# A decoder step on one Trainium2 core: the convolution's running sum in PSUM, and layer A's weight residues on GpSimd

## The chip, the cores and the metric

The kernel runs on one core of a Trainium2 chip. The core has a matrix engine (TensorE, PE in the profile, its weight loads PEld), a vector engine (VectorE, DVE), a scalar engine (ScalarE, ACT), a general engine (GpSimd, POOL), and a queue engine (SyncE, SP) that issues DMAs. Each engine has its own instruction queue; semaphores order work between them. Matrix products land in PSUM (eight banks of 128 x 512 floats), everything else lies in SBUF. The metric is the device time of one launch in microseconds, the median of several runs. Smaller is better.

## What is computed

One inference step of a small decoder trunk, for 512 prompt tokens and 64 sample tokens (8 sequences of 8), 576 columns together, width 2048. Layer A is a Conformer convolution module, layer B a dilated sliding-window attention; both also attend to a memory of 256 positions. This is layer A:

```python
h = jnp.einsum('btd,de->bte', x, w_in)          # w_in: 2048 x 5632
ga, gb, gate, qm, gm = jnp.split(h, ...)        # 1536, 1536, 1536, 512, 512
u = ga * jax.nn.sigmoid(gb)
ext = jnp.concatenate([conv_prev, u], axis=1)   # 30 older rows ahead
conv = depthwise_conv(ext, w_dw, width=31) + b_dw
c = silu(layernorm(conv)) * silu(gate)
m = mem_attn(qm, mem_kv) * silu(gm)
y = jnp.einsum('bte,ed->btd', jnp.concatenate([c, m], -1), w_out)
x = layernorm(ALPHA * x + y)
```

Layer B is built in the same way, with attention in place of the convolution, and adds its relative-position bias from a table (`rel_bias`) to the logits.

## The kernel before

**Products in three passes.** Weights and activations are float32. Each is split into a high part, rounded to a format that TensorE multiplies in one pass, and a low part, the residue. A product is high x high + high x low + low x high. Activations are split once. Weights arrive from HBM as slabs: a *unit* is one slab of 128 output channels by all inputs, a *quarter* is 4 of its 16 blocks of 128 inputs (a 128x512 tile). For each quarter ScalarE writes the high part (`wh`, line 203, five buffers) and VectorE the low part (`wl = raw - wh`, line 214, four buffers).

**Order.** The program is written out by hand: on each engine, instructions run in the order in which the Python code issues them. `run_steps` (line 241) goes through the list of quarters. A step issues the quarter's matmuls (line 262), then hooks, then the high part of the quarter three steps ahead and the low part of the one two steps ahead (`issue_split`), then the evacuation of a unit that ended in the step before, then `stage_lanes` (line 219, one piece from each of three queues of generators), then *background* work from `bg`. How much background work a step issues is a budget, `state["avail"]`: a step adds the time of its columns, and each piece takes off a planned cost; a low part takes 0.6.

**Layer A's sequence** (line 26): 12 pairs of units gb and ga (`p`), 4 units qm, 8 memory units (`mk`, 256 columns), 4 gm, one gate, up to `n_seq` (line 790); then the other gates, then the output projection. At the end of ga number j, `ev_ga` (line 612) writes `ep` and `es` on VectorE, stores `es` to the output `o_cs` by a DMA from GpSimd's queue (line 622), and appends the convolution of 128 channels to `bg`: `first` (line 647), then 30 `tap`s (line 656). A tap is one VectorE instruction on 128x512, `conv = ep[k:] * w + conv` (line 662), in place in SBUF.

**The bias tables.** A hook at step 20, the first memory quarter, puts `bias_task` (line 517) into lane 2. All its DMAs go through GpSimd's queue: it fills two tables in HBM (lines 529 to 536), stores the rows of three groups four times each (line 550), and then for each of four heads copies them in shifted rows. The core of that is:

```python
for r in range(4):
    nc.gpsimd.dma_start(dram(tp_, o, ...), dram(sc[0], ...))            # line 557
    nc.gpsimd.dma_start(tp_[h, r, 0:32, 0:128], md[0:32, 0:128])        # line 559, over part of the same rows
...                                                                     # line 561, twice
yield
nc.gpsimd.dma_start(dram(tl_, o, ...), dram(sc[0], ...))                # line 567
...                                                                     # line 570, three times
yield
...                                                                     # lines 574 (twice) and 577
yield
```

**PSUM.** `pp` (two buffers of two banks) takes the units' products. `at` (line 101, four buffers of one bank) takes all small products: memory attention, transposes, sums over channels, bias rows.

Of the kernel before, what the change touches and what calls it, by code (L numbers as in the profile page):

```python
# [13 lines left out]
AF = mybir.ActivationFunctionType  # L14
OP = mybir.AluOpType
# [4 lines left out]
TP, TS = 512, 64  # L20
# [14 lines left out]
TAPS = 31  # L35
# [46 lines left out]
def trunk(ctx, tc, xt, memt, wm, wa, wao, wb, wbo, cst, scv, kc, rest, mc, relb, oneh,  # L82
          o_y, o_yf, o_cp, o_cs, o_kv, o_kvn, o_kc, o_rest, o_mem):
    nc = tc.nc
# [8 lines left out]
    def u(shape, dt=F32, name="u"):  # L93
        names[0] += 1
        return U.tile(list(shape), dt, tag="u", name=f"{name}{names[0]}")
# [5 lines left out]
    def at(shape=(128, 512)):  # L101
        names[0] += 1
        return psum.tile(list(shape), F32, tag="at", bufs=4, name=f"at{names[0]}")

    def cast(ap):
        return ap.bitcast(F32)
# [33 lines left out]

    steps, quarters, halves = [], [], []
    raws, splits = {}, {}
    state = dict(dma=0, hi=0, split=0, pos=0, avail=0.0, extra=0.0, cap=4.0)
    lanes = [deque(), deque(), deque()]
    bg = deque()
    hooks = {}
# [44 lines left out]
    def issue_hi(upto):  # L191
        while state["hi"] < min(upto, len(quarters)):
            i = state["hi"]
            un, q, hidx = quarters[i]
            issue_dma(hidx + 1)
            r = raws[hidx][q % 2]
            if un.keep:
                f_ = un.keep
                hi, lo = f_([128, 512], F32R, "keep"), f_([128, 512], F32R, "keep")
            else:  # L200
                hi = wpool.tile([128, 512], F32R, tag="wh", bufs=5, name=f"wh{i}")
                lo = None
            nc.scalar.copy(hi, r)  # L203
            splits[i] = (hi, lo, r)
            state["hi"] += 1

    def issue_split(upto):
        while state["split"] < min(upto, len(quarters)):
            i = state["split"]
            issue_hi(i + 1)  # L210
            hi, lo, r = splits[i]
            if lo is None:
                lo = wpool.tile([128, 512], F32R, tag="wl", bufs=4, name=f"wl{i}")
            nc.vector.tensor_tensor(lo, r, cast(hi), op=OP.subtract)  # L214
            splits[i] = (hi, lo)
            state["split"] += 1
            state["avail"] -= 0.6

    def stage_lanes():
        for ln in lanes:  # L220
# [72 lines left out]
    def cols(ps, n=288):  # L293
        return ps[:, :, 0:n]
# [295 lines left out]
    def sp_x(k):  # L590
        xh[k], xl[k] = split_f32r(xraw.pop(k), [128, T], "x")

    def x_ready(k, c):
        if xh[k] is None:
            sp_x(k)
# [4 lines left out]
    later, cst_ = {}, {}  # L600
# [10 lines left out]
    def ev_ga(j):  # L611
        def f(ps):
            ep = u([128, HIST + TP], name="ep")
            es = u([128, 8, HIST + 8], name="es")
            nc.vector.memset(ep[:, 0:HIST], 0.0)
            nc.sync.dma_start(es, scv[j])
            g = sg.pop(j)
            nc.vector.tensor_tensor(ep[:, HIST:].rearrange("p (c n) -> p c n", c=2), cols(ps, 256),
                                    g[:, 0:TP].rearrange("p (c n) -> p c n", c=2), op=OP.mult)
            nc.vector.tensor_tensor(es[:, :, HIST:], ps[:, 1, 256:320].rearrange("p (b s) -> p b s", b=8),  # L620
                                    g[:, TP:].rearrange("p (b s) -> p b s", b=8), op=OP.mult)
            nc.gpsimd.dma_start(o_cs[j], es)
            cv = convs[j] = u([128, T], name="conv")
            cs = cv[:, TP:]
            prod = {}

            def sample_tap(k, bias=None):

                g = min(k // 8, 3)
                if g not in prod:  # L630
                    prod[g] = u([128, 9, TS], name="prod")
                dst = prod[g][:, k - 8 * g + (1 if g else 0), :].rearrange("p (b s) -> p b s", b=8)
                w = dw[:, j * 31 + k:j * 31 + k + 1]
                if bias is None:
                    nc.scalar.activation(dst, es[:, :, k:k + 8], AF.Copy, scale=w)  # L635
                else:
                    nc.scalar.activation(dst, es[:, :, k:k + 8], AF.Identity, scale=w, bias=bias)

            def sample_sum(g):
                n = 9 if g in (1, 2) else 8  # L640
                if g == 0 and j > 1:
                    nc.scalar.activation(prod[0][:, 8, :], cst_["shift"][:, TP:], AF.Copy, scale=-1.0)
                    n = 9
                dst = cs if g == 3 else prod[g + 1][:, 0, :]
                nc.vector.reduce_sum(dst, prod.pop(g)[:, 0:n, :].rearrange("p k n -> p n k"), axis=AX.X)

            def first():
                w = dw[:, j * 31:j * 31 + 1]
                b = b_dw[:, j:j + 1]
                if j < 2:  # L650
                    nc.vector.tensor_scalar(cv[:, 0:TP], ep[:, 0:TP], w, b, op0=OP.mult, op1=OP.add)
                    return
                nc.scalar.activation(cv[:, 0:TP], cst_["shift"][:, 0:TP], AF.Identity, bias=b, scale=-1.0)
                nc.vector.scalar_tensor_tensor(cv[:, 0:TP], ep[:, 0:TP], w, cv[:, 0:TP], op0=OP.mult, op1=OP.add)

            def tap(k):
                w = dw[:, j * 31 + k:j * 31 + k + 1]
                for m in range((k - 4) * TAPS // 27, (k - 3) * TAPS // 27) if k >= 4 else ():
                    sample_tap(m, None if m else b_dw[:, j:j + 1])
                if k == 6:  # L660
                    nc.scalar.copy(cps[:, j, :], ep[:, TP:TP + HIST])
                nc.vector.scalar_tensor_tensor(cv[:, 0:TP], ep[:, k:k + TP], w, cv[:, 0:TP], op0=OP.mult, op1=OP.add)  # L662
            bg.append((0.67, first))
            rest_ = later.pop(j - 1, [])
            for k in range(1, TAPS):
                bg.append((0.67, lambda k=k: tap(k)))
                if k in (13, 20, 28):
                    bg.append((0.7, lambda g=(k - 12) // 7: sample_sum(g)))
                if k in (3, 5, 7, 9, 11) and rest_:
                    bg.append(rest_.pop(0))  # L670

            def shift():

                ps_ = colsum(cv)
                cst_["shift"] = u([128, T], name="shift")
                for c in range(2):
                    nc.vector.tensor_scalar(cst_["shift"][:, c * 288:(c + 1) * 288], ps_[c][:, :288], 1.0 / 128, None,
                                            op0=OP.mult)
                yield 0.75

            def shifted():
                nc.vector.tensor_tensor(cv, cv, cst_["shift"], op=OP.subtract)

            def square():
                cst_["sq"] = u([128, T], name="sq")
                nc.scalar.activation(cst_["sq"], cv, AF.Square)
                if j == 0:
                    cst_["s1"] = u([128, T], name="s1")
                    nc.vector.tensor_copy(cst_["s1"], cv)
                    cst_["s2"] = cst_.pop("sq")  # L690
                else:
                    nc.vector.tensor_tensor(cst_["s1"], cst_["s1"], cv, op=OP.add)

            def square2():
                nc.vector.tensor_tensor(cst_["s2"], cst_["s2"], cst_.pop("sq"), op=OP.add)
            last_sum = (0.7, lambda: sample_sum(3))
            todo = later[j] = [last_sum]
            if j == 0:
                todo.append((0.0, lambda: lanes[2].append(shift())))
            if j < 2:  # L700
                todo.append((0.67, shifted, lambda: "shift" in cst_))
            todo.append((0.67, square))
            if j:
                todo.append((0.67, square2))
        return f
# [64 lines left out]
    for it in seq:  # L770
# [11 lines left out]
        un = Unit(wa[row + j], KT, xh, xl, ch, ev(j), x_ready, cost=0.75 if kind == "ga" else 0.0)  # L782
# [6 lines left out]
        if kind == "ga" and j == NCT - 1:  # L789
            n_seq = len(steps)  # L790
# [698 lines left out]
    for e in range(KT - N_SPLIT, KT):  # L1489
# [3 lines left out]
        un = unit_last(e, [(FIRST, T - FIRST)], ev, 1.2)  # L1493
# [10 lines left out]
    n_end = len(steps)  # L1504


    def temp_pool():
        es_ = ExitStack()
        scopes["s"] = (es_, es_.enter_context(tc.tile_pool(name="spool2", bufs=4)))
# [14 lines left out]
        hooks.setdefault(n_mk - 10 + j, []).append(lambda j=j: sp_mem(j))  # L1524
    for k in range(4, KT):
        hooks.setdefault((k - 4) // 4 * 2 + 1, []).append(lambda k=k: x_ready(k, None))
    temp_pool()
    issue_dma(1)
    for k in range(KT):
# [181 lines left out]
```

## Time and profile before

| | us |
|---|---|
| median of 3 runs | 1817.6 |
| lowest, highest | 1812.64, 1824.57 |
| the profiled execution, device time | 1815.19 |
| its span, first to last instruction | 1813.4 |

The profile is one execution. Busy time says how long an engine was executing, an idle stretch is put down to what ended it, and the chain that ended last is followed back from the last instruction. On that chain TensorE has 97% of the span, of which the line of the units' matmuls (262) has 86%. VectorE is busy for 55%, ScalarE for 37%, GpSimd for 7%. In 40 slices of the span VectorE's busy tenths are 6 to 9 in the first 14 and 2 to 6 in most of the others.

### The profile page before, as it was taken

The page shows a single profiled execution, that of the slowest core. Times are in us where ns is not written, and L with a number is a line of the kernel's source. Part 1 is how long each engine was busy: PE and PEld are TensorE (multiplying, and loading weights), DVE is VectorE, ACT ScalarE, POOL GpSimd, SP SyncE. Part 2 cuts the span into 40 slices and gives each one's busy share as a digit, 9 for nine tenths or more (in the row PEclk, how much of TensorE's full clock was granted, in tenths as well). Part 3 has the DMA queues.
Part 4 walks back from the last instruction along what each step waited for, and adds up shares of the span by engine and source line. Part 5 has one row for each costly group of instructions (what it writes and reads, how often), then busy time and mean ns, then how long its engine had stood idle before and what let it go on. Part 6 is the DMA issues. An engine that isn't in the chain of part 4 may idle for free.

```text
span 1813.4 us, 34545 instructions
## 1 busy us (share of the span) xinstructions
PE 1799.5 (99%) x14374; PEld 1725.0 (95%) x14374; DVE 1003.8 (55%) x1739; ACT 670.9 (37%) x1544; POOL 119.9 (7%) x215
## 2 busy tenths in 40 slices
PE   8999999999999999999999999999999999999998
PEld 8999999999999999999999999988999988899997
DVE  6977988378999765546762233222322222225866
ACT  5454444355455442223562232222322212224334
POOL 0222221000000000000000000010000011100000
PEclk9999999999999999999999999999999999999999
DMA  8585777575655465565642343676566666842312
GB/s 304 182 265 169 233 231 268 173 244 189 207 197 194 155 223 187 171 224 206 198 157 82 117 140 117 210 247 250 186 214 223 198 241 232 286 158 60 115 48 105
DMA packets 83901, 344.87 MB, mean 190 GB/s; under 512 B 15823, under 2 KB 24047, under 8 KB 72352
## 3 DMA queue, kind: packets, MB, share of 16 engines
q1 hardware_dynamic: 60240, 249.48, 41.3%
q0 software_dynamic: 20048, 90.03, 14.1%
q10 hardware_dynamic: 3456, 3.15, 0.5%
q8 instruction: 113, 1.85, 0.4%
q14 instruction: 44, 0.36, 0.1%
HBM read 322.83 MB, written 114.42 MB: 241 GB/s over the span
## 4 chain that ended last, share of the span: by engine, by line
PE 97%; ACT 1%; DMA 1%; DVE 1%; issue 0%; ACTq 0%; SPq 0%; DVEq 0%
PE pp L262 86%; PE at L1203 1%; PE at L1148 1%; PE at L458 1%; PE at L436 1%; DMA raw<-wb 1%; PE at L1085 1%; PE at L1083 1%; PE at L503 0%; PE at L483 0%; PE at L1106 0%; PE at L451 0%; PE pp L880 0%; PE at L804 0%; PE at L1096 0%; PE at L1053 0%
## 5 line engine op out<-in xcount | busy, mean ns | idle before, releaser
L214 DVE TENSOR_TENSOR wl<-raw,wh 128x512 fp32r<-128x512 f32 x492 | 333.7, 687 | 295.6 <-PE pp L262 159.3
L203 ACT CAST wh<-raw 128x512 fp32r<-128x512 f32 x492 | 297.7, 618 | 492.5 <-PE pp L262 168.0
L262 PE MATMUL pp<-yh,wh 128*128 128x320 f32 (+2 forms) x1536 | 340.8, 304 | 0.0
L262 PE MATMUL pp<-yl,wh 128*128 128x320 f32 (+2 forms) x1536 | 329.5, 296 | 0.3 <-DVE yl L997 0.3
L262 PE MATMUL pp<-yh,wl 128*128 128x320 f32 (+2 forms) x1536 | 329.3, 296 | 0.0
L262 PE MATMUL pp<-xh,wh 128*128 128x288 f32 (+2 forms) x1408 | 307.5, 300 | 5.8 <-ACT xh L364 5.8
L262 PE MATMUL pp<-xh,wl 128*128 128x288 f32 (+2 forms) x1408 | 303.4, 297 | 0.0
L262 PE MATMUL pp<-xl,wh 128*128 128x288 f32 (+2 forms) x1408 | 303.4, 297 | 0.0
L262 PEld LDWEIGHTS pp<-yh,wh 128*128 128x128 f32 x1536 | 253.2, 189 | 27.7 <-ACT wh L203 13.4
L662 DVE SCALAR_TENSOR_TENSOR conv<-ep,consts,conv 128x512 f32<-128x512 f32 x360 | 269.7, 749 | 6.9
L262 PEld LDWEIGHTS pp<-yl,wh 128*128 128x128 f32 x1536 | 256.0, 189 | 0.7 <-DVE yl L997 0.7
L262 PEld LDWEIGHTS pp<-yh,wl 128*128 128x128 f32 x1536 | 256.0, 189 | 0.0
L262 PEld LDWEIGHTS pp<-xh,wh 128*128 128x128 f32 x1408 | 234.2, 191 | 8.9 <-ACT xh L364 5.8
L262 PEld LDWEIGHTS pp<-xl,wh 128*128 128x128 f32 x1408 | 234.1, 190 | 0.3 <-DVE xl L365 0.3
L262 PEld LDWEIGHTS pp<-xh,wl 128*128 128x128 f32 x1408 | 234.1, 190 | 0.0
L262 PE MATMUL pp<-cath,wh 128*128 128x288 f32 (+2 forms) x640 | 140.5, 297 | 0.0
L262 PE MATMUL pp<-catl,wh 128*128 128x288 f32 (+2 forms) x640 | 139.7, 296 | 0.0
L262 PE MATMUL pp<-cath,wl 128*128 128x288 f32 (+2 forms) x640 | 139.6, 296 | 0.0
L262 PEld LDWEIGHTS pp<-cath,wh 128*128 128x128 f32 x640 | 104.2, 189 | 0.8 <-issue 0.3
L262 PEld LDWEIGHTS pp<-catl,wh 128*128 128x128 f32 x640 | 104.1, 189 | 0.0
L262 PEld LDWEIGHTS pp<-cath,wl 128*128 128x128 f32 x640 | 104.1, 189 | 0.0
L635 ACT ACTIVATE prod<-es,consts 128x64 f32<-128x64 f32 x360 | 103.0, 343 | 1.3 <-ACT mkv L403 1.3
(281 smaller groups left out, 1838.3 us busy)
## 6 DMA issues: line engine op xcount, KB each, us to landing
o_kc<-kc SPq DMA_DIRECT2D x104, 512.0 KB, 5.7
kv<-kc POOLq DMA_DIRECT2D x52, 1024.0 KB, 5.4
raw<-wb SPq DMA_DIRECT2D x96, 512.0 KB, 4.1
raw<-wa SPq DMA_DIRECT2D x86, 512.0 KB, 4.5
o_rest<-rest SPq DMA_DIRECT2D x64, 512.0 KB, 6.3
kv<-mc POOLq DMA_DIRECT2D x16, 1024.0 KB, 6.9
raw<-wao SPq DMA_DIRECT2D x32, 512.0 KB, 4.5
raw<-wm SPq DMA_DIRECT2D x24, 512.0 KB, 4.8
```

Of the source, the lines that this page charges most:

```text
L203: nc.scalar.copy(hi, r)
L214: nc.vector.tensor_tensor(lo, r, cast(hi), op=OP.subtract)
L262: nc.tensor.matmul(un.ps[:, c, :n], w[wi], xs[k][:, c0:c0 + n], start=(k == 0 and a == 0), stop=(k == un.nk - 1 and a == 2 and not un.tail))
L436: nc.tensor.matmul(lg[:, a * 256:(a + 1) * 256], q[:, t0:t0 + 128], kt, start=True, stop=True)
L458: nc.tensor.matmul(o[:, 0:256], vt[:, kk, :], PT[:, kk * 256:(kk + 1) * 256], start=(kk == 0), stop=(kk == 1))
L635: nc.scalar.activation(dst, es[:, :, k:k + 8], AF.Copy, scale=w)
L662: nc.vector.scalar_tensor_tensor(cv[:, 0:TP], ep[:, k:k + TP], w, cv[:, 0:TP], op0=OP.mult, op1=OP.add)
L1083: nc.tensor.matmul(o, lhs, kk, start=True, stop=True, tile_position=(0, 32 * a))
L1085: nc.tensor.matmul(lg[:, 128 + 128 * g:256 + 128 * g], q_[g, h][:, r * 128:(r + 1) * 128], k_[g, h][:, r * 128:(r + 1) * 128], start=True, ...
L1148: nc.tensor.matmul(lg[32 * rg:32 * rg + 32, :], qe[g][:, rg * 128 + b * 32:rg * 128 + b * 32 + 32], ck[:, rg, :], start=(b == 0), stop=(b ...
L1203: nc.tensor.matmul(acc[32 * rg:32 * rg + 32, 0:128], pe[i % 2][:, rg * 128 + b * 32:rg * 128 + b * 32 + 32], cv[:, rg * 4 + b, :], start=( ...
```

## The change

- `conv`'s running sum is kept in a tile of `at`, one PSUM bank, from `first` to the last tap, which writes its result to the SBUF tile `conv`. `first`, on ScalarE and VectorE, writes PSUM too.
- `issue_split` issues the subtraction for the first `state["low"]` quarters on GpSimd in place of VectorE, and then takes nothing off `avail`. `halves_before(n_seq)` is the number of quarters up to `n_seq`.

```diff
-    state = dict(dma=0, hi=0, split=0, pos=0, avail=0.0, extra=0.0, cap=4.0)
+    state = dict(low=0, dma=0, hi=0, split=0, pos=0, avail=0.0, extra=0.0, cap=4.0)
...
-            nc.vector.tensor_tensor(lo, r, cast(hi), op=OP.subtract)
+            if i < state["low"]:
+                nc.gpsimd.tensor_tensor(lo, r, cast(hi), op=OP.subtract)
+            else:
+                nc.vector.tensor_tensor(lo, r, cast(hi), op=OP.subtract)
+                state["avail"] -= 0.6
             splits[i] = (hi, lo)
             state["split"] += 1
-            state["avail"] -= 0.6
...
+            acc = {}
...
             def first():
                 w = dw[:, j * 31:j * 31 + 1]
                 b = b_dw[:, j:j + 1]
+                ac = acc[0] = at()
                 if j < 2:
-                    nc.vector.tensor_scalar(cv[:, 0:TP], ep[:, 0:TP], w, b, op0=OP.mult, op1=OP.add)
+                    nc.vector.tensor_scalar(ac, ep[:, 0:TP], w, b, op0=OP.mult, op1=OP.add)
                     return
-                nc.scalar.activation(cv[:, 0:TP], cst_["shift"][:, 0:TP], AF.Identity, bias=b, scale=-1.0)
-                nc.vector.scalar_tensor_tensor(cv[:, 0:TP], ep[:, 0:TP], w, cv[:, 0:TP], op0=OP.mult, op1=OP.add)
+                nc.scalar.activation(ac, cst_["shift"][:, 0:TP], AF.Identity, bias=b, scale=-1.0)
+                nc.vector.scalar_tensor_tensor(ac, ep[:, 0:TP], w, ac, op0=OP.mult, op1=OP.add)
...
-                nc.vector.scalar_tensor_tensor(cv[:, 0:TP], ep[:, k:k + TP], w, cv[:, 0:TP], op0=OP.mult, op1=OP.add)
+                dst = acc[0] if k < TAPS - 1 else cv[:, 0:TP]
+                nc.vector.scalar_tensor_tensor(dst, ep[:, k:k + TP], w, acc[0], op0=OP.mult, op1=OP.add)
...
+    def halves_before(n):
+
+        return max(un.qi[q] for un, q, _, _ in steps[:n]) + 1
...
+    state["low"] = halves_before(n_seq)
```

## Rows read from the trace of the kernel before

**Rows 1.** The page, section 1: busy us, share of the span, instructions by engine.

```profile
PE 1799.5 (99%) x14374; PEld 1725.0 (95%) x14374; DVE 1003.8 (55%) x1739; ACT 670.9 (37%) x1544; POOL 119.9 (7%) x215
```

**Rows 2.** Waits of TensorE, whole span: waiter, releaser, us in total, times, longest.

```profile
PE pp L262 <- ACT xh L364: 5.8, 1, 5.8
PE pp L262 <- DVE wl L214: 1.2, 2, 1.0
PE at L388 <- ACT mkv L403: 0.7, 1, 0.7
```

**Rows 3.** Groups by line and shape, VectorE: busy us, mean ns, idle before.

```profile
L214 DVE TENSOR_TENSOR wl<-raw,wh 128x512 fp32r<-128x512 f32 x492 | 333.7, 687 | 295.6 <-PE pp L262 159.3 <-ACT wh L203 101.6 <-issue 34.3
L662 DVE SCALAR_TENSOR_TENSOR conv<-ep,consts,conv 128x512 f32<-128x512 f32 x360 | 269.7, 749 | 6.9
...
L890 DVE SCALAR_TENSOR_TENSOR r<-xl,r 128x576 f32<-128x576 f32 x15 | 11.4, 758 | 0.5
...
L889 DVE SCALAR_TENSOR_TENSOR r<-xh,pp 128x576 f32<-128x576 f32 x15 | 11.3, 755 | 31.1 <-PE pp L262 31.1
```

**Rows 4.** Windows: us, busy (instructions) PE PEld DVE ACT POOL, PEclk, DMA, GB/s.

```profile
115.00:120.00 5.00, 3.92 (x20) 3.72 (x21) 4.96 (x8) 3.34 (x9) 1.22 (x2) 0.70 0.39 93
...
150.00:200.00 50.00, 50.00 (x378) 50.00 (x377) 45.54 (x68) 21.71 (x62) 12.40 (x20) 1.00 0.63 201
450.00:500.00 50.00, 50.00 (x378) 50.00 (x377) 49.29 (x74) 22.43 (x66) 1.09 (x2) 1.00 0.62 206
```

**Rows 5.** Timeline of GpSimd: start us, us, what [idle before, and what ended it].

```profile
66.26 0.53 POOL L529 MEMSET mt<- 128x512 f32 x1
...
73.99 0.53 POOL L536 DMA_DIRECT2D tl__92<-md  x1
85.82 2.16 POOL L550 DMA_DIRECT2D bd<-bt  x4 [11.30 <-ACT bt L546]
...
94.84 0.74 POOL L557 DMA_DIRECT2D tp__91<-bd  x1 [0.19 <-issue]
...
120.89 0.50 POOL L559 DMA_DIRECT2D tp__91<-md  x1 [3.73 <-DMA tp__91<-bd]
...
123.62 0.57 POOL L567 DMA_DIRECT2D tl__92<-bd  x1
136.94 1.70 POOL L570 DMA_DIRECT2D tl__92<-bd  x3 [12.74 <-DMA tl__92<-bd]
...
144.81 0.72 POOL L557 DMA_DIRECT2D tp__91<-bd  x1
...
197.21 0.52 POOL L559 DMA_DIRECT2D tp__91<-md  x1 [3.11 <-DMA tp__91<-bd]
...
220.96 1.70 POOL L570 DMA_DIRECT2D tl__92<-bd  x3 [6.49 <-DMA tl__92<-bd]
225.70 1.09 POOL L574 DMA_DIRECT2D tl__92<-bd  x2 [3.04 <-DMA tl__92<-bd]
...
275.23 2.20 POOL L622 DMA_DIRECT2D o_cs<-es  x4
```

**Rows 6.** Waits of GpSimd, 60 to 280 us.

```profile
POOL tp__91 L559 <- DMA tp__91<-bd: 82.9, 16, 8.4
POOL tl__92 L570 <- DMA tl__92<-bd: 34.9, 4, 12.7
...
POOL tl__92 L574 <- DMA tl__92<-bd: 17.0, 4, 6.1
```

**Rows 7.** Groups by line, GpSimd.

```profile
L125 POOL MEMSET qe<- 128x512 f32 x3 | 1.4, 524 | 0.0
```

**Rows 8.** The chain that ended last, 60 to 135 us: start us, us, what.

```profile
90.01 17.47 PE pp L262 x144
```

**Rows 9.** Timeline of VectorE: `es` of the third pair.

```profile
153.58 0.21 DVE L620 TENSOR_TENSOR es<-pp,sg 128x64 f32<-128x64 f32 x1
```

**Rows 10.** Timeline of SyncE's queue: the first copies of `rest`.

```profile
121.20 13.03 SPq L354 DMA_DIRECT2D o_rest<-rest  x6
```

## The prediction

> **What bounds the kernel now.** I read the page first, for shares by engine. TensorE's matmuls fill 99% of the span [rows 1], so the question is only whether something holds it up. The waits of TensorE come next: 5.8 us on the first cast of x, 1.2 us in all on VectorE's low parts, 0.7 us on a small product, nothing else of size [rows 2]. So the 333.7 us that VectorE spends on low parts [rows 3] are almost wholly hidden. Then the windows: in a stretch of plain quarters TensorE gets through 378 matmuls in 50 us whether VectorE is busy for 45.5 us of it or for 49.3 [rows 4]; at 24 matmuls to a quarter that is 3.17 us a quarter. VectorE is nearly full there, and still not the bound.
>
> The view that decides is the last one I read, GpSimd's timeline, because a second engine is about to be put on TensorE's supply line. GpSimd is busy for only 119.9 us [rows 1], but what matters in an in-order queue is when it is blocked. From 94.84 to 275.23 us it works through one chain, the copies of the bias tables (lines 557 to 577): issue a DMA, wait until it has landed, issue the next one onto the same rows. In its first head the copies of line 567 (123.62) are followed by a wait of 12.74 us; the second head begins at 144.81 [rows 5]. Of these 180.4 us, 82.9 + 34.9 + 17.0 = 134.8 us are such waits [rows 6], and the other 45.6 us are issuing. Now it costs nothing, since only o_cs stores and later loads stand behind it.
>
> **What is taken from VectorE.** `low` is the number of quarters up to `n_seq`: 12 pairs of ga and gb (96 quarters), qm, gm and one gate (36), and the 8 memory units (32), together 164. So 164 subtractions of 687 ns [rows 3], 112.7 us, leave VectorE, and `avail` is no longer charged 0.6 for each. TensorE waited 1.2 us for them in the whole run, so what can be won is that 1.2 us and part of the lull at 115 to 120 us, where 20 matmuls ran in 5 us [rows 4] against the 38 of the usual pace (18 x 0.13 = 2.4 us).
>
> **The running sum in PSUM.** 360 taps of 749 ns [rows 3], with 12 first terms, now read and write a PSUM bank. Reading: the two lines 889 and 890 are the same operation on 128x576, one with its second input in PSUM and one wholly in SBUF, and take 755 and 758 ns [rows 3]: no surcharge. [...] Writing PSUM from VectorE is in no row; I bound it between nothing and the 62 ns by which line 662 exceeds line 214, the largest surcharge between two-input rows of 512 columns [rows 3]. I take nothing; at the upper bound 372 x 0.062 = 23 us go back to VectorE, less than the 112.7 it is rid of. One of the four `at` banks is now held for 31 taps at a time; users of the other three are the memory attention's small matmuls, whose readers run a step ahead.
>
> **The subtraction on GpSimd.** No row shows a two-input operation there. The nearest is its MEMSET of 128x512, 524 ns [rows 7], one write and no input. I bound the subtraction from below by this and from above by three such passes (two reads, one write), 1.57 us, and take the middle, 1.1 us. A plain quarter leaves 3.17 us, so it keeps up there. A quarter of a memory unit leaves 1.46 us (144 matmuls, which are 12 quarters of 12, in 17.47 us [rows 8]), so it just keeps up there too; at 1.57 us the 19 memory quarters outside the chain would cost 2 us.
>
> **What stands in front of it.** This is where the change costs. A low part is issued two steps ahead of its quarter, and `stage_lanes` runs behind it in the same step. `bias_task` joins lane 2 at step 20, the first memory quarter, and gives out one piece a step. Counting its yields, GpSimd's queue becomes: low 28, the fill of `md` and eight copies, low 29, four bias stores, low 30, four, low 31, four, low 32, then for each of four heads the piece of line 557 to 561 (four waits), a low part, lines 567 and 570 (one wait), a low part, lines 574 and 577 (one wait), a low part; the last piece stands before low 44. Each quarter's third pass needs its low part, so TensorE may not pass quarter 33 until head 1's first piece is through, and so on. That the queue doesn't let later work by is in the rows: `es` of the third pair was written at 153.58 us [rows 9], yet the stores of pairs three to six were issued back to back at 275.23 us, as soon as the chain had ended [rows 5].
>
> The price, first part: the fill piece takes from 66.26 to 74.52 us, 8.3 us, and the bias stores 12 x 0.54 = 6.5 us [rows 5]; their wait for ScalarE before 85.82 us falls away, since by then TensorE has passed that product. With four subtractions (4.4) this is 19.2 us, while TensorE has four quarters of 1.46 (5.8) and a lead: with four `wl` buffers GpSimd is at most three quarters ahead, less the subtraction, 3.3 us. Stall 10 us.
>
> Second part, the chain: 45.6 us of issuing plus the waits. How long are those, when TensorE crawls? The smallest of each kind in the trace are 3.11 us (line 559), 6.49 (line 570) and 3.04 (line 574) [rows 5]; 16 x 3.11 + 4 x 6.49 + 4 x 3.04 = 88 us against 134.8. They were measured under traffic of some 200 GB/s [rows 4]. In the stalled stretch there is next to none: twelve quarters of weights (256 KB each) in some 140 us are 22 GB/s, and the o_rest copies, first issued at 121.20 us [rows 10], belong to steps behind the memory units. So I go near the smallest, 90 us, and the chain takes 135.6. Of the 12 subtractions in it, the two thirds that stand in front of a wait run while that DMA lands, so they add 4 x 1.1 = 4.4. TensorE does its 12 quarters within, 17.5 us. Stall 135.6 + 4.4 - 17.5 = 122.5 us.
>
> [...]
>
> Sum, against the profiled execution: 1815.2 + 10 + 122.5 = 1947.7, say 1948 us. The median of the three runs is 2.4 us above that execution, which is nothing beside the bounds. Everything behind `n_seq` stays as it is, later.
>
> Bounds of the unknown: waits as long as before and no subtraction hidden, 10 + 180.4 + 13.2 - 17.5 = 186 us, 2001 us; waits half their smallest (44), 10 + 45.6 + 44 + 4.4 - 17.5 = 87 us, 1902 us. With no wait at all, issuing alone would still be 45.6 + 13.2 - 17.5 = 41 us.
>
> **Rivals.** *The waits don't shrink* (the copies with their many short rows are slow by themselves): 2001 us. For it, between 115 and 120 us traffic was down to 93 GB/s [rows 4], and the wait of line 559 that ended at 120.89 us still took 3.73 us [rows 5]; against it, that is already below their mean of 82.9 / 16 = 5.2 [rows 6]. *They shrink far more*: 1902 us.
>
> *The shared port.* Taps with both tensors in SBUF and a GpSimd subtraction may block each other. With the sum in PSUM a tap has one SBUF input left. If it still shut out and was shut out by the subtraction, VectorE would get 1.1 us per quarter back for the 0.69 it lost; in the stretch where it is full (from 450 us on, the last 47 quarters or so before `n_seq` [rows 4]) it would fall 19 us behind, o_cs would hold the low parts behind it, and the time would be 1967 us. Nothing in the trace of before shows the two together. [...]
>
> *The other side: the low parts are not held up*, because the queue lets them pass the waiting copies, or because the pieces end up elsewhere. Then only the gains remain, 1815.2 - 1.2 - 2.4 = 1812 us, no change that can be measured. It would need the copies to take less than the 17.5 us that TensorE has for the twelve quarters; their issuing alone takes 45.6, and the stores at 275.23 us speak against passing.
>
> **How the numbers follow.** The forecast (a stall of 105 to 170 us) 0.63; waits unshrunk 0.13; far shorter waits 0.11; the port on top of the stall 0.06; no stall 0.07. The predicted time is the forecast's, 1948 us. The range runs from a little below the short waits to a little above the unshrunk ones, 1895 to 2010, and leaves out the last case and part of the port. About 1% is what a measurement of this kernel can tell from no change: slower by over 1% 0.93, within 1% 0.05, faster 0.02.
>
> **What would show it.** Right: between roughly 90 and 230 us TensorE idle for over 100 us, waiting for GpSimd's `wl`, and GpSimd waiting for DMAs of lines 559, 570 and 574 in between; the quarter pace of 3.17 us before and behind it; the granted clock low inside. Wrong: TensorE's waits for `wl` near zero, or `wl` written in time while the bias copies are pending; then the order in the queue is not what I counted. If the subtraction takes over 3.2 us, all of layer A is paced by it, and the time is far above the range. If taps are longer than 811 ns, writing PSUM costs more than I allow.

## The result, and the profile after

The changed kernel takes 1954.97 us (median of 4 executions, 1949.19 to 1966.91), the kernel before in the same session 1815.74. The ratio is 1.0767, 95% interval 1.0703 to 1.0831: slower by 139 us. The prediction was 1948, in a range of 1895 to 2010. The profiled execution of the changed kernel is the longest of its four; the last section says where its last 10 us went.

The page of the changed kernel, busy time by engine, and two rows of its 40 slices (compare [rows 1]):

```profile
PE 1831.9 (93%) x14374; PEld 1747.4 (89%) x14374; DVE 921.9 (47%) x1575; ACT 671.6 (34%) x1544; POOL 336.8 (17%) x379
...
PE   8932299999999999999999999999999999999999
...
PEclk9955599999999999999989999999999999999997
```

VectorE is busy for 82 us less, GpSimd for 217 more, and no engine is anywhere near full except TensorE. The loss stands in slices 3 to 5, 98 to 246 us: there TensorE is busy for 2 or 3 tenths. The waits of TensorE and of GpSimd (waiter, releaser, us in total, times, longest) say for what:

```profile
PE pp L265 <- POOL wl L215: 114.0, 15, 21.7
PE pp L265 <- ACT xh L367: 6.5, 2, 6.3
PE pp L265 <- DVE wl L217: 3.1, 3, 1.9
```

```profile
POOL tp__91 L562 <- DMA tp__91<-bd: 59.0, 16, 5.0
POOL o_cs L625 <- DVE es L623: 49.4, 9, 14.0
...
POOL tl__92 L573 <- DMA tl__92<-bd: 20.4, 4, 5.8
...
POOL tl__92 L577 <- DMA tl__92<-bd: 1.3, 2, 0.7
```

TensorE, which in [rows 2] waited for nothing of size, now waits 114 us for low parts written by GpSimd; GpSimd in turn stands at the same waits for landed copies as in [rows 6] (lines 559, 570 and 574 are now 562, 573 and 577). GpSimd's timeline puts the two together (start, duration, what, idle before and what ended it):

```profile
95.63 0.55 POOL L536 DMA_DIRECT2D tl__92<-md  x1 [5.27 <-DMA md<-mt]
...
111.18 0.74 POOL L560 DMA_DIRECT2D tp__91<-bd  x1
116.94 0.51 POOL L562 DMA_DIRECT2D tp__91<-md  x1 [5.01 <-DMA tp__91<-bd]
...
133.35 1.27 POOL L215 TENSOR_TENSOR wl<-raw,wh 128x512 fp32r<-128x512 f32 x1
134.55 0.58 POOL L570 DMA_DIRECT2D tl__92<-bd  x1
140.72 1.70 POOL L573 DMA_DIRECT2D tl__92<-bd  x3 [5.59 <-DMA tl__92<-bd]
142.44 1.27 POOL L215 TENSOR_TENSOR wl<-raw,wh 128x512 fp32r<-128x512 f32 x1
143.85 1.11 POOL L577 DMA_DIRECT2D tl__92<-bd  x2
...
252.03 8.75 POOL L215 TENSOR_TENSOR wl<-raw,wh 128x512 fp32r<-128x512 f32 x7
```

Between 111.18 and 133.35 us GpSimd issues a copy, waits, issues the next, four times, and not one low part. At 133.35 it does one, at 142.44 one. At 252.03 the chain is over, and seven follow at once. Two windows (us, busy and instructions of PE PEld DVE ACT POOL, PEclk, DMA share, GB/s), one inside the stall, one behind it:

```profile
220.00:240.00 20.00, 0.10 (x1) 0.00 (x0) 0.00 (x0) 0.70 (x2) 6.19 (x9) 0.50 0.14 43
300.00:350.00 50.00, 50.00 (x377) 50.00 (x376) 41.67 (x56) 24.73 (x74) 20.67 (x18) 1.00 0.62 200
```

In 20 us one matmul record, VectorE idle, the granted clock at 0.50; behind it 377 matmuls in 50 us at a granted clock of 1.00, the pace of [rows 4].

Where the time came in can be read off ScalarE's timeline, from the start of the same evacuation in each kernel (us; differences to the kernel before in brackets; the experiments are told below):

| evacuation | before | after | e9_charge | e3_spread | e10_spread_mem | e8_late_spread |
|---|---|---|---|---|---|---|
| first qm, ahead of the memory units | 72.69 | 74.53 (+1.8) | 74.25 (+1.6) | 74.03 (+1.3) | 73.05 (+0.4) | 73.64 (+1.0) |
| first gb behind them | 140.17 | 276.11 (+135.9) | 270.56 (+130.4) | 159.09 (+18.9) | 156.99 (+16.8) | 134.33 (-5.8) |
| the gate of layer A | 435.41 | 571.95 (+136.5) | 565.50 (+130.1) | 454.91 (+19.5) | 452.05 (+16.6) | 435.26 (-0.2) |
| 65 us later | 500.71 | 642.80 (+142.1) | 630.80 (+130.1) | 525.79 (+25.1) | 523.70 (+23.0) | 500.56 (-0.2) |
| a gate at 1021 | 1021.47 | 1163.44 (+142.0) | 1147.39 (+125.9) | 1045.93 (+24.5) | 1042.66 (+21.2) | 1019.87 (-1.6) |
| end of the span | 1813.4 | 1965.1 (+151.7) | 1949.6 (+136.2) | 1848.2 (+34.8) | 1842.7 (+29.3) | 1811.7 (-1.7) |

In e8_late_spread the bias work comes behind the memory units, so its second row is early. In the changed kernel 1.8 us come in the start, 134.1 in the memory units, 6 more between the row behind them and the gate at 1021, and in this execution 10 in the tail. The row "65 us later" already shows these 6, but there it is ScalarE that is late: TensorE is busy for 70.57 of the 70.85 us between 571.95 and 642.80. It loses time just behind, where it waits three times, 3.1 us in all, for VectorE's low parts (line 217, between 636 and 690 us).

Last, the groups (busy us, mean ns, idle before) that answer to [rows 3]; lines 368 and 701 took 756 and 752 ns before, and the two instructions of line 656 (the first term of the first two convolutions) 540:

```profile
L215 POOL TENSOR_TENSOR wl<-raw,wh 128x512 fp32r<-128x512 f32 x164 | 217.0, 1330 | 196.9 <-PE pp L265 103.2 <-ACT wh L203 74.9 <-ACT prod L639 9.9
...
L668 DVE SCALAR_TENSOR_TENSOR at<-ep,consts,at 128x512 f32<-128x512 f32 x348 | 262.2, 754 | 8.9
L217 DVE TENSOR_TENSOR wl<-raw,wh 128x512 fp32r<-128x512 f32 x328 | 222.2, 687 | 269.7 <-PE pp L265 159.0 <-ACT wh L203 83.9 <-issue 26.4
L368 DVE TENSOR_TENSOR xl<-xraw,xh 128x576 fp32r<-128x576 f32 x16 | 16.6, 1090 | 13.9 <-ACT xh L367 13.9
...
L701 DVE TENSOR_TENSOR sq<-sq,sq 128x576 f32<-128x576 f32 x11 | 11.0, 999 | 0.0
...
L656 DVE TENSOR_SCALAR at<-ep,consts 128x512 f32<-128x512 f32 x2 | 1.6, 803 | 0.0
```

A tap takes 754 ns with its sum in PSUM, 749 before. Lines 368 and 701 read two tensors from SBUF and run where GpSimd subtracts; both became longer on the mean, 1090 ns in place of 756 and 999 in place of 752.

### The profile page after: what moved, and what is told of

It is laid out like the page before. It is cut to its first block, busy times and chain, and to the rows that moved or that the text cites. A ratio compares the mean times of both kernels' runs of the same rounds, so it can differ in the third digit from the quotient of the medians.

```text
span 1965.1 us, 34661 instructions
## 1 busy us (share of the span) xinstructions
PE 1831.9 (93%) x14374; PEld 1747.4 (89%) x14374; DVE 921.9 (47%) x1575; ACT 671.6 (34%) x1544; POOL 336.8 (17%) x379
## 4 chain that ended last, share of the span: by engine, by line
PE 82%; DMA 7%; DVE 5%; POOL 2%; issue 1%; ACT 1%; SPq 0%; ACTq 0%; POOLq 0%; DVEq 0%
PE pp L265 72%; DMA tp__91<-bd 3%; DVE at L668 3%; PE at L1209 1%; DMA tl__92<-bd 1%; PE at L1154 1%; POOL wl L215 1%; DMA raw<-wa 1%; DMA raw<-wb 1%; PE at L461 1%; PE at L439 1%; DVE prod L649 1%; PE at L1091 1%; PE at L810 0%; PE at L1089 0%
## 5 line engine op out<-in xcount | busy, mean ns | idle before, releaser
L217 DVE TENSOR_TENSOR wl<-raw,wh 128x512 fp32r<-128x512 f32 x328 | 222.2, 687 | 269.7 <-PE pp L265 159.0
L265 PEld LDWEIGHTS pp<-yh,wh 128*128 128x128 f32 x1536 | 252.7, 189 | 27.7 <-issue 13.0
L668 DVE SCALAR_TENSOR_TENSOR at<-ep,consts,at 128x512 f32<-128x512 f32 x348 | 262.2, 754 | 8.9
L215 POOL TENSOR_TENSOR wl<-raw,wh 128x512 fp32r<-128x512 f32 x164 | 217.0, 1330 | 196.9 <-PE pp L265 103.2
L265 PE MATMUL pp<-memh,wl 128*128 128x256 f32 x256 | 83.1, 325 | 113.7 <-POOL wl L215 113.7
L265 PEld LDWEIGHTS pp<-memh,wl 128*128 128x128 f32 x256 | 57.3, 224 | 117.6 <-POOL wl L215 117.5
L332 POOL DMA_DIRECT2D kv<-mc x16 | 8.8, 554 | 584.4 <-DVE wl L217 376.3
```

What stands on the lines that cost most here:

```text
L215: nc.gpsimd.tensor_tensor(lo, r, cast(hi), op=OP.subtract)
L265: nc.tensor.matmul(un.ps[:, c, :n], w[wi], xs[k][:, c0:c0 + n], start=(k == 0 and a == 0), stop=(k == un.nk - 1 and a == 2 and not un.tail))
L332: nc.gpsimd.dma_start(t_, src)
L668: nc.vector.scalar_tensor_tensor(dst, ep[:, k:k + TP], w, acc[0], op0=OP.mult, op1=OP.add)
```

## The experiments

The theory: GpSimd's queue is in order, so each low part waits for the bias copies in front of it and for their landing; the stall is that chain less the work that TensorE had to do meanwhile. Rivals: GpSimd is just too slow for the memory quarters; the shared port; the PSUM sum.

**One part alone: the sum in PSUM (e1_psum_only).** The line that sets `low` is left out, so that all low parts stay on VectorE.

```diff
-    state["low"] = halves_before(n_seq)
```

> One part alone: the running sum in PSUM, every low part on VectorE and charged to the budget as before. Theory (the queue: all of the loss comes from low parts that stand behind the bias copies in GpSimd's queue): 1812 to 1825 us, no change that can be measured, taps at 750 to 760 ns. Rival (the bank held for 31 taps, or the write into PSUM, costs something): over 1835 us, with TensorE waiting for small products of the memory attention.

Measured: 1816.94 against 1815.89 us, ratio 1.0004 (0.9978 to 1.0030). The taps take 752 ns. Waits of TensorE:

```profile
PE pp L265 <- ACT xh L367: 5.9, 1, 5.9
PE pp L265 <- DVE wl L217: 1.1, 2, 0.9
```

They are those of [rows 2]. By itself the PSUM sum does nothing: the whole loss comes in with the subtraction.

**The other part alone: the subtraction on GpSimd, the sum in SBUF (e2_sub_only).**

```diff
-                ac = acc[0] = at()
+                ac = acc[0] = cv[:, 0:TP]
```

> The other part alone: low parts on GpSimd, the running sum in SBUF as before. Theory (the queue): the same stall as with both parts, 1945 to 1975 us, and over 105 us of TensorE waiting for GpSimd's low parts. Rival (the shared port): taps now read two SBUF tensors, so tap and subtraction shut each other out; taps would take over 900 ns on the mean, VectorE would fall behind by about 1 us a quarter, and the time would be over 1985 us.

Measured: 2000.84 us, ratio 1.1009 (1.0966 to 1.1051). The theory's 1945 to 1975 was missed; longer taps and subtractions, as the rival has it, came on top of the stall. Their groups:

```profile
L668 DVE SCALAR_TENSOR_TENSOR conv<-ep,consts,conv 128x512 f32<-128x512 f32 x360 | 368.4, 1023 | 9.3
...
L215 POOL TENSOR_TENSOR wl<-raw,wh 128x512 fp32r<-128x512 f32 x164 | 239.7, 1473 | 183.0 <-ACT wh L203 108.9 <-PE pp L265 59.8 <-PE at L454 10.8
```

A tap with two SBUF inputs takes 1023 ns here, with one of them in PSUM 754; the subtraction too is longer, 1473 ns in place of 1330. So the two halves of the change belong together: the PSUM sum, worth nothing alone, is worth 46 us (2000.84 - 1954.97) once the low parts are on GpSimd.

**Spreading the waits (e3_spread).** `bias_task` gets a lane of its own, and between a copy and the next one that waits for it stand three to five steps (`GAP`), so that low parts are issued while it lands.

```diff
+GAP = 3
...
-    lanes = [deque(), deque(), deque()]
+    lanes = [deque(), deque(), deque(), deque()]
...
+                for _ in range(GAP):
+                    yield
                 nc.gpsimd.dma_start(tp_[h, r, 0:32, 0:128], md[0:32, 0:128])
...
-    hooks.setdefault(20, []).append(lambda: lanes[2].append(bias_task()))
+    hooks.setdefault(20, []).append(lambda: lanes[3].append(bias_task()))
```

> Both parts, but the bias task has a lane of its own and gives out each copy that waits for an earlier one three steps later, so that the earlier one has landed when GpSimd comes to it. No wait is taken away, only what makes it last. Theory (the queue): GpSimd's waits for landings fall from 84 us to under 20, TensorE's waits for low parts from 114 to under 20 us, 1812 to 1840 us. Rival (GpSimd is simply too slow for this, or its subtractions and VectorE hold each other up): 1900 us or more.

Measured: 1845.72 us, ratio 1.0142 (1.0092 to 1.0193), 109 us less than the changed kernel and 6 above the expected range. Waits and two windows:

```profile
PE pp L266 <- POOL wl L216: 10.8, 9, 3.5
...
POOL tl__92 L580 <- DMA tl__92<-bd: 8.6, 1, 8.6
...
POOL tp__91 L567 <- DMA tp__91<-bd: 5.4, 3, 2.8
```

```profile
80.00:100.00 20.00, 16.86 (x122) 15.38 (x122) 19.22 (x26) 12.82 (x38) 18.02 (x20) 0.91 0.70 216
...
120.00:140.00 20.00, 16.20 (x130) 15.39 (x129) 0.00 (x0) 7.99 (x16) 18.41 (x19) 1.00 0.72 213
```

The same instructions in the same queue, with low parts put between a copy and the one that waits for it: TensorE's wait falls from 114.0 to 10.8 us. The table's +17.6 between its first two rows come from the memory units, where GpSimd is now nearly full, 18 of 20 us, and TensorE busy for 16 to 17 of 20. Not all of it is GpSimd's rate: one landing still holds the queue up, for 8.6 us (line 580, at 143 to 152 us). How the 17.6 us divide between the two is not shown.

**The same with the sum in SBUF (e4_spread_sbuf).** The edit of the second experiment on top of this one.

> As the spread kernel, with the running sum back in SBUF: only the port is left to differ. If two SBUF inputs and a reading GpSimd shut each other out: taps over 900 ns on the mean, subtractions longer than 1330 ns, and at least 10 us above the spread kernel. If not: taps near 750 ns and within 5 us of the spread kernel.

Measured: 1901.91 us, ratio 1.0459 (1.0419 to 1.0499), 56 us more than with the sum in PSUM.

```profile
L676 DVE SCALAR_TENSOR_TENSOR conv<-ep,consts,conv 128x512 f32<-128x512 f32 x360 | 374.7, 1041 | 9.3
```

With most of the stall gone the price of the second SBUF input stands alone: 360 taps longer by 0.29 us are 103 us of VectorE's time, and the subtractions take 1442 ns on the mean, 1329 in e3_spread. The two together make the time 56 us longer.

**The chain beside longer quarters (e5_hook52).** `bias_task` joins at step 52, behind the memory units, in place of 20.

```diff
-    hooks.setdefault(20, []).append(lambda: lanes[2].append(bias_task()))
+    hooks.setdefault(52, []).append(lambda: lanes[2].append(bias_task()))
```

> The change with one number altered: the bias task starts at step 52, the first plain quarter behind the memory units, in place of step 20. Its copies and their waits are the same; TensorE now has 3.17 us of work for each quarter that stands between them, in place of 1.46. Theory (the queue): the stall is chain and first part (141 + 20 us) less 16 quarters of 3.17 and a lead of 8, about 102 us, so 1915 to 1945 us. Rival (GpSimd can't keep up in the memory quarters): that part is unchanged, so 1945 us or more, with the waits for low parts before step 52.

Measured: 1931.02 us, ratio 1.0624 (1.0581 to 1.0668). The copies' waits are the same (58.0 us at line 562), TensorE waits 86.3 us for low parts. Beside the chain and its first part TensorE now has sixteen quarters of 3.17 us in place of 1.46, and a lead of 8 us in place of 3.3: by the sum of the expectation the gain should be 32 us. TensorE's wait falls by 27.7, the time by 23.9. And the memory units, with all their low parts on GpSimd but no copies in its queue, now pass unhindered: from 80 to 100 us and from 120 to 140 us TensorE is busy for 20.00 of 20 us, GpSimd for 18.63 and 12.04. Neither the memory quarters nor GpSimd's rate make the stall; the chain does.

**One wait in place of four (e6_wait_once).** Within each head the four copies come first, then the four that go over part of their rows.

```diff
                 nc.gpsimd.dma_start(dram(tp_, o, ...), dram(sc[0], ...))
+            for r in range(4):
                 nc.gpsimd.dma_start(tp_[h, r, 0:32, 0:128], md[0:32, 0:128])
```

> The change, with the four copies of line 560 of a head issued first and the four of line 562 behind them, the same eight transfers. Each of line 562 still waits for its own forerunner, but the four landings overlap. Theory (the queue, and in it the landings): GpSimd's waits of line 562 fall from 59 us to about 12, and the time by as much, 1898 to 1920 us. Rival (it is the issuing and the subtractions that hold TensorE up, not the waits): within 10 us of the change, 1945 us or more.

Measured: 1914.73 us, ratio 1.0515 (1.0482 to 1.0549).

```profile
PE pp L265 <- POOL wl L215: 63.5, 15, 9.9
...
POOL tp__91 L563 <- DMA tp__91<-bd: 11.2, 6, 3.0
```

The copies' wait falls from 59.0 to 11.2 us, 47.8 less, TensorE's by 50.5, and the time by 40.2. No instruction was added or taken away: the stall follows the waits in the queue.

**The memory units' low parts left on VectorE (e7_vec_mem).** These are quarters 24 to 51, all of the memory units but the first.

```diff
-            if i < state["low"]:
+            if i < state["low"] and not 24 <= i < 52:
```

> The change, but the low parts of quarters 24 to 51, the memory units, go back to VectorE. So TensorE gets through the memory units unhindered, while the bias copies still stand in GpSimd's queue, now in one block ahead of low part 52. Theory (the queue): one single wait of TensorE at quarter 52, of some 105 to 130 us, and 1920 to 1950 us in all, although not one low part stands between the copies. Rival (the memory quarters are too short for a subtraction of 1.33 us on GpSimd): the stall is gone, 1815 to 1835 us.

Measured: 1941.37 us, ratio 1.0673 (1.0642 to 1.0704). TensorE's timeline, then GpSimd's:

```profile
246.52 0.85 PE L265 MATMUL pp<-xh,wl 128*128 128x256 f32 x2 [119.72 <-POOL wl L215]
```

```profile
244.60 0.58 POOL L580 DMA_DIRECT2D tl__92<-bd  x1
245.19 4.96 POOL L215 TENSOR_TENSOR wl<-raw,wh 128x512 fp32r<-128x512 f32 x4
```

The fifteen waits have become one of 119.72 us (and one of 0.4), at the first quarter whose low part is behind the chain. GpSimd as too slow an engine is out here too: the quarters in question are not its own any more.

**The stall taken away altogether (e8_late_spread).** As with the spread waits, but with `GAP = 2`, `bias_task` joining at step 52, GpSimd's low parts beginning there, and the budget charged 0.45 for each.

```diff
+GAP = 2
...
-            if i < state["low"]:
+            if 52 <= i < state["low"]:
                 nc.gpsimd.tensor_tensor(lo, r, cast(hi), op=OP.subtract)
+                state["avail"] -= 0.45
...
-    hooks.setdefault(20, []).append(lambda: lanes[2].append(bias_task()))
+    hooks.setdefault(52, []).append(lambda: lanes[3].append(bias_task()))
```

> What the theory makes of it: both parts of the change for the plain quarters behind the memory units alone (52 to the end of the sequence), the bias task started there, in a lane of its own, each waiting copy two plain steps (6.3 us) behind the one it waits for, and a low part on GpSimd charged 0.45 to the budget, so that VectorE does not fall behind. Theory: TensorE's waits for low parts under 4 us, 1808 to 1820 us, as before or slightly below. Rival (GpSimd's part costs something even when nothing blocks its queue): 1825 us or more.

Measured: 1818.59 us against 1816.82, ratio 1.0003 (0.9979 to 1.0027). TensorE has no wait for GpSimd left, and 112 subtractions are off VectorE:

```profile
PE pp L267 <- DVE wl L219: 0.2, 1, 0.2
```

Even so nothing is won. TensorE was the bound before, and 77 us less work for VectorE (112 x 0.687) shorten a wait of 1.2 us.

**The budget (e9_charge).** The changed kernel, with 0.45 taken off `avail` for each low part on GpSimd.

```diff
                 nc.gpsimd.tensor_tensor(lo, r, cast(hi), op=OP.subtract)
+                state["avail"] -= 0.45
```

> The changed kernel, but a low part on GpSimd takes 0.45 off the budget for background work (it took nothing). Theory: in the changed kernel TensorE's work behind the convolutions was 6 us further back than behind the memory units (offset to the kernel before +142.1 against +136.5), because the budget, no longer charged for 164 quarters, gave VectorE more taps per step than it could do, so that es came late, and o_cs held the low parts on GpSimd. If so, the stall in front of the bias copies stays as it was (waits of TensorE for wl 105 to 115 us), the offset stays within 2 us between 435 and 530 us of the kernel before, and the time is 3 to 8 us less, 1946 to 1952 us. Rival: the 6 us come from the subtraction itself or from the port; then the offset grows by 4 us or more all the same, and the time is that of the changed kernel, 1952 to 1960 us.

Measured: 1950.52 us against 1825.12, ratio 1.0702 (1.0658 to 1.0747); TensorE waits 109.4 us for low parts. In the table the 6 us between 435 and 501 us are gone (+130.1 and +130.1). The other kernels of the table agree: e8_late_spread, which charges 0.45 too, gains nothing between these two rows (-0.2 and -0.2), while e3_spread and e10_spread_mem, which charge nothing, gain 5.6 and 6.4. So the 6 us came from the budget: uncharged, it gave VectorE more taps in a step than it could do. In the changed kernel VectorE's taps hold 43.5% of the chain that ended last between 560 and 690 us, and TensorE waits 3.1 us for VectorE's own low parts, here 0.2; the way through `o_cs` and GpSimd that the expectation names is not shown. The chain of copies also begins earlier, at 103.76 us in place of 111.18, and the offset falls by another 4 us before 1021; why is open. The medians differ by 4.5 us, the two profiled executions by 15.6, and the intervals of the two kernels overlap; the table's rows, one execution of each kernel, carry this verdict, not the times.

**Spread waits, the first 52 low parts left on VectorE (e10_spread_mem).** Only `low` differs from the third experiment: `if 52 <= i < state["low"]`.

> As e3_spread (waiting copies spread over the steps, fourth lane), but the first 52 quarters' low parts, the memory units' among them, stay on VectorE. Theory: of the 30 us that e3_spread is above the kernel before, about 19 come from the memory quarters, 1.46 us each, in which GpSimd had 1.33 us of subtraction and the issuing of the bias copies, and 2 from the start; then the time is 1820 to 1828 us, and what is left is the lag late in the sequence. Rival: the bias copies still hold up low parts later on, or the convolutions lag by more; then 1835 us or more.

Measured: 1839.2 us against 1825.12 (the session of these two experiments, in which the kernel before had a higher median), ratio 1.0095 (1.0060 to 1.0130): the rival's side. The timelines of TensorE and GpSimd:

```profile
142.29 0.85 PE L266 MATMUL pp<-xh,wl 128*128 128x256 f32 x2 [17.92 <-POOL wl L216]
```

```profile
111.36 0.52 POOL L567 DMA_DIRECT2D tp__91<-md  x1 [9.09 <-DMA tp__91<-bd]
...
132.94 0.51 POOL L567 DMA_DIRECT2D tp__91<-md  x1 [13.44 <-DMA tp__91<-bd]
...
140.28 0.58 POOL L575 DMA_DIRECT2D tl__92<-bd  x1
140.94 3.74 POOL L216 TENSOR_TENSOR wl<-raw,wh 128x512 fp32r<-128x512 f32 x3
```

With VectorE writing the low parts, TensorE goes through the memory units at full pace, busy for 20.00 of 20 us from 80 to 100 and from 100 to 120 us; the steps put in between are too short to cover a landing (9.09 us for the first copy, beside 292 GB/s between 100 and 120 us, and 13.44 for the third), and GpSimd's first low part stands behind the copies once more. The step of that theory which failed: it took the copies' waits as gone because they were short in the third experiment, where GpSimd itself had slowed the steps down.

## Why the prediction was right

**The order in the queue** held as counted: the low part at 133.35 us stands behind the first head's four waits, the next behind one. e6 and e3 show it causally, by 40 and 109 us.

**The second part.** From the first copy (111.18) to the seven subtractions (252.03) are 140.85 us; predicted were 135.6 + 4.4 = 140.0. Within it two terms were off against each other. The waits come to 59.0 + 20.4 + 1.3 = 80.7 us, not 90: line 562 waits 3.7 us on the mean (smallest before 3.11 [rows 5]), but line 577 almost never, since a low part runs in front of it while its DMA lands. The rest, 60.2 us, is issuing and all the eleven subtractions between these two times (45.6 + 11 x 1.33 = 60.2), not 45.6 + 4.4. I had taken two thirds of the subtractions as hidden behind a landing. Only one of the three in each head stands between a copy and the one that waits for it (at 142.44, between lines 573 and 577); the other two stand ahead of the copy that is waited for (at 133.35 ahead of line 570, and the one ahead of the next head), and hide nothing. So subtractions cost some 10 us more than predicted and waits 9 us less, and that the two cancel is luck.

**The first part.** The offset in this stretch is 134.1 us; less 140.85 - 17.5 it leaves 10.8, predicted 10. The sum says no more than that the two fit; the fill's wait at line 536, for instance, was in its 8.3 us with the 2.70 us that it took before, and took 5.27.

**The subtraction** takes 1.33 us, between the bounds of 0.52 and 1.57, above the 1.1 taken. In the stall this hardly matters; in e3 it does, where GpSimd has 1.33 us and its issuing to do in each 1.46 us quarter.

**The waits shrink** when TensorE crawls: 5.2 us before, 3.7 after at line 562, beside 66 GB/s over the chain (43 in the window above) in place of some 200 [rows 4]. The traffic was not as low as the 22 GB/s predicted, and the waits of line 562 not as short as the smallest before. In e10_spread_mem, beside 292 GB/s, they are long again, 9.09 us for the first. The rival *the waits don't shrink* (2001 us) is out.

**PSUM.** No surcharge, as taken, for a tap, which reads one input from PSUM and writes PSUM: 754 against 749 ns over 348 taps, 1.7 us. Writing is another matter for one kind of instruction. I had allowed at most 62 ns; the two TENSOR_SCALAR of the first terms (line 656), which read SBUF and now write PSUM, take 803 ns in place of 540, and 806 in e1, where GpSimd subtracts nothing. That they are two makes it 0.5 us in all; in a kernel with many of them, at 263 ns each, it would count.

**The port.** The rival put it on a tap with one SBUF input, and there it is not (754 ns with GpSimd subtracting beside it). With two it is: 1023 ns in e2 and 1041 in e4, and the subtractions take 1473 and 1442 ns in place of 1330. That it is a port which the two share is the rival's reading; the runs show the times alone.

**Where it was wrong.** "Everything behind `n_seq` stays as it is, later", and the start at no cost. Both failed, by 6 and 1.8 us, about the distance between 1948 and the 1955 measured. The 6 were the budget (e9): I had read that `avail` is no longer charged and counted it as a gain alone. The 1.8 us go with line 368, which makes the low part of x at the start: 1090 ns in place of 756, two SBUF inputs beside GpSimd's first subtractions. In e10, without those, the start is 0.4 us later; but e8, also without them, shows 1.0, and in e9 and e3 the line takes 1189 and 1187 ns while the start is only 1.6 and 1.3 us later. So how much of the 1.8 is line 368 stays open. What GpSimd's subtractions do to a two-input operation had been weighed for the taps alone, not for the others that run beside GpSimd.

**The other side** (1812 us, no stall) needed the copies not to stand in front. e8 made that case by hand and came out at 1818.59, no different from before: the gains named there, 1.2 and 2.4 us, are below what can be measured.

## What to carry to other kernels

Before moving work to an engine that looks idle, read that engine's timeline for what it waits for where the moved work will stand: GpSimd was 7% busy, and a queue blocked for 81 us on landing copies stopped TensorE for 114. A copy that must wait for another copy is best issued several steps later, or batched so that one wait covers four; here that alone is worth 40 to 109 us. And relief for an engine that isn't the bound is worth only the waits that this engine caused the bound, here 1.2 us of 1815, however many microseconds of work are moved.

## What was not expected of the hardware

The size of the mutual slowing: a 128x512 tap is 270 to 290 ns longer, and the subtraction 110 to 140 ns longer, when both of the tap's tensors are in SBUF, over whole runs in which GpSimd subtracts in part of the time only.

The tail. In the profiled execution the granted clock falls in the last 30 us, while TensorE goes on working:

```profile
1910.00:1930.00 20.00, 20.00 (x151) 18.44 (x150) 15.28 (x37) 7.29 (x16) 0.00 (x0) 1.00 0.21 75
1930.00:1950.00 20.00, 20.00 (x87) 14.01 (x85) 11.62 (x32) 8.13 (x18) 0.00 (x0) 0.70 0.31 111
1950.00:1965.00 15.00, 10.41 (x23) 5.49 (x22) 3.75 (x10) 3.27 (x6) 0.00 (x0) 0.50 0.19 70
```

By the table, from the gate at 1021 to the end takes 791.9 us before and 791.8 in e8, where the clock stays up (mean of the window from 1800 to 2000 us 0.99 in both), and 801.7, 802.2 and 802.3 in after, e9 and e3, where it falls (0.93, 0.92 and 0.92). That is probably no property of the change: of 17 executions of the kernel before, 11 had a mean granted clock of 0.997 to 1.000 and took 1812.9 to 1818.1 us, and 6 had 0.991 or 0.992 and took 1822.0 to 1826.2. That one in three of them loses the same 10 us in the tail is an inference; no such execution of the kernel before was profiled, and what makes the clock fall is open.
